# Eleven rows of unused matmuls behind the third weight tile of a two-layer hybrid encoder

## The chip, the cores and the metric

The kernel runs on one core of a Trainium2 chip, in one launch. The metric is the device time in microseconds of that core; lower is better. The engines are PE (matrix multiply; PEld is its loading of weights), DVE and ACT (vector and scalar work), POOL, and SP, which issues the transfers. All of them run their own queue in order and wait for each other by semaphores.

## The reference

Two layers are computed over 528 tokens (16 learned ones ahead of 512) of width 1024. Each layer is a SwiGLU feed forward, a mixer of three groups of heads, and a second SwiGLU feed forward, each with a residual and a layer norm.

```python
def swiglu(h, w_in, w_out):
    gate, up = jnp.split(h @ w_in, 2, axis=-1)
    return (jax.nn.silu(gate) * up) @ w_out
...
    for l in range(DEPTH):
        h = layer_norm(DEEPNORM_ALPHA * h + 0.5 * swiglu(h, w_ff1_in[l], w_ff1_out[l]), ln_g[l, 0], ln_b[l, 0])
        mix = hybrid_mixer(h * valid, w_in[l], w_out[l], ...)
        h = layer_norm(DEEPNORM_ALPHA * h + mix, ln_g[l, 1], ln_b[l, 1])
        h = layer_norm(DEEPNORM_ALPHA * h + 0.5 * swiglu(h, w_ff2_in[l], w_ff2_out[l]), ln_g[l, 2], ln_b[l, 2])
    return h[:, CHUNK:]
```

The mixer runs gated DeltaNet, RWKV-7 and retention heads side by side, all from one input projection, with one output projection. The feed forward has an inner width of 2816, which is 22 blocks of 128.

## The kernel before

The stream lies transposed: features on partitions, tokens along columns. The tokens are worked in two halves, of 272 and of 256 columns (`NH`). A half of the stream is a tile of 128 partitions x 8 blocks x 272 columns; the 256-column half uses 256 of the 272 columns of each block, so its blocks begin 272 columns apart too.

Products are made almost as exactly as in float32 from three matmuls of the type fp32r. Every operand is split by ACT and DVE into a rounded part (`hi`) and the rest (`lo`); ACT writes the first and DVE subtracts. `mm3` (L165) then runs, for each of 8 blocks of the inner dimension, high x high, high x low and low x high: 24 matmuls into one PSUM bank per weight tile. A weight tile is 128 x 1024 floats, 512 KB, loaded by SP into `raw` (4 slots) and split by `load_w` into `whl` (3 slots), in two pieces of 128x512 each on ACT and on DVE. A slot of `whl` comes free when the last matmul that reads it has run.

The units of work of the first feed forward alternate: a `gate` tile, whose result goes through a tanh on ACT (L127) and a product on DVE (L118), and an `up` tile, whose result is multiplied to it and split into `ghi` and `glo`. After eight pairs, eight `ffo` tiles add to the residual. At the start of the program 12 matmuls of ones (`warm`, float32, which appear as 24 in the trace) run, then the first weight tile is loaded and the input with it, four pieces of two blocks each, split as they arrive. `u[0]` is the first unit, and `run_half(u[1:s1], 0)` with `s1 = 3` runs the second and third.

The order of the instructions on each engine isn't written by hand: a tile scheduler places them by its own simulation of the program, with the order of the code as priority, so a unit's matmuls may be placed among those of another. The mixer's small matmuls (`pS`, `pyt`, `pG` and so on, plain float32) are placed among the feed forward's in that way.

Of the kernel before, what the change touches and what calls it, by code (L numbers as in the profile page):

```python
# [14 lines left out]
PSUM = bass.MemoryType.PSUM  # L15
DRAM = bass.MemoryType.DRAM

L = 2
T = 528
NMAX = 272  # L20
NH = (272, 256)
# [5 lines left out]
RSQRT = (-0.49999807, 0.375001003, -0.314047223, 0.273950612)  # L27
# superchunks of a half: (first column, tokens, chunks, tokens per chunk, slot)
SUPERS = (
# [5 lines left out]

# columns of the constants
_C = {}
# [6 lines left out]

# columns of the parameters that lie along partitions
_P = {}
# [13 lines left out]
def body(ctx, tc, xT, w1i, w1o, w2i, w2o, win, wba, wout, par, wsm, wupx, cst, tab, out):  # L60
# [15 lines left out]

    # rings of scratch tiles: (columns, slots); what runs side by side has rings of its own
    RINGS = {
# [53 lines left out]
    def rsqrt(v, n, rows=128, new=TI):  # L132
        """v**-0.5 of a small tile: y from the exponent's halving, within 3.5%, times e**-0.5 for e = v y**2,
        whose polynomial around e = 1 is right to 3e-8."""
        t, y, p = (new(n, x)[:rows] for x in ("rt", "ry", "rp"))
        ts(V, y.bitcast(I32), v.bitcast(I32), -0.5, ALU.mult, float(0x5F3759DF), ALU.add)
        tt(V, t, y, y, ALU.mult)
        tt(V, t, t, v, ALU.mult)
        ts(V, p, t, -1.0, ALU.add, RSQRT[3], ALU.mult)
        ts(V, t, t, -1.0, ALU.add)  # L140
        for c in RSQRT[2::-1]:
            stt(p, p, c, t, ALU.add, ALU.mult)
        stt(y, p, 1.0, y, ALU.add, ALU.mult)
        return y
# [22 lines left out]

    S = {}  # tiles that live across steps

    nh, off = list(NH), [0, 0]  # columns at work, and those of the half before them  # L170

# [6 lines left out]

    # ---------------------------------------------------------------- layer norm
    def add_r(hf, m):  # L180
# [69 lines left out]

    # ---------------------------------------------------------------- feed forward
    def ff_units(l, wi, wo, j, last=False):
        """One unit per weight tile: (tile's source, k-tiles, work of a half)."""
        units = []
# [107 lines left out]

    # ---------------------------------------------------------------- mixer inputs
    def silu2(dst, x, n, src=None):
        """2 * silu(x)"""
        t = ring("ws", n, name="tanh")
        act(t, x, AF.Tanh, scale=0.5)
        stt(dst, t, 1.0, x, ALU.add, ALU.mult)

    def in_units(l):  # L370
# [20 lines left out]
        def conv(i):  # L391
            def run(hf, w):
                n = nh[hf]
                ps = bank(psA, "qkv")[:, :n]
                mm3(ps, w, S["hl", hf], 8)
                p = ring("ws", n + 3, name="pc")
                act(p[:, 3:], ps, AF.Copy)
                if hf == 0:
                    G.memset(p[:, 0:3], 0.0)
                    G.tensor_copy(halo[:, i], p[:, n: n + 3])  # L400
                else:
                    G.tensor_copy(p[:, 0:3], halo[:, i])
                c = ring("ws", n, name="conv")
                c0 = _P["conv"][0] + 4 * i
                act(c, ps, AF.Identity, scale=P[:, c0 + 3: c0 + 4])
                for tap in (0, 1, 2):
                    stt(c, p[:, tap: tap + n], P[:, c0 + tap: c0 + tap + 1], c, ALU.mult, ALU.add)
                # heads' k and q lie side by side
                if i < 4:
                    d = keep(hf, "qk")[:, 2 * i + 1, :n]  # L410
                elif i < 8:
                    d = keep(hf, "qk")[:, 2 * (i - 4), :n]
                else:
                    d = keep(hf, "vz")[:, i - 8, :n]
                silu2(d, c, n)
            return (win[l, i], 8, run)

        def rw(i):
            def run(hf, w):
                n = nh[hf]  # L420
# [14 lines left out]
                if i in (4, 5):  # L435
                    # v: the two chunks of a superchunk change places
                    c = ring("ws", n, name="vmix")
                    act(c, ps, AF.Identity, scale=S["par2"][:, i: i + 1])
                    for s, _, nch, Cn, _ in SUPERS[hf]:
                        for q in range(nch):  # L440
                            a, b = s + q * Cn, s + (nch - 1 - q) * Cn
                            stt(d[:, b: b + Cn], p[:, a: a + Cn], mu, c[:, a: a + Cn], ALU.mult, ALU.add)
                else:
                    act(d, ps, AF.Identity, scale=S["par2"][:, i: i + 1])
                    stt(d, p[:, 0:n], mu, d, ALU.mult, ALU.add)
# [39 lines left out]

    # ---------------------------------------------------------------- inverses of I + M
    def inverse_base(dg, dw, nch, Cn):
        """M: strict upper triangles, four heads' in dg, four in dw; inverses of all eight,
        of the 16-wide blocks on the diagonals here."""
        BS = 16  # L490
# [13 lines left out]

        # blocks on the diagonal, one to a partition
        key = "md" if nch == 2 else "md0"
# [35 lines left out]
    def inverse_levels(out, M, X, Y, nch):  # L542
        """From 16-wide blocks to whole chunks."""
        if Y is None:
# [30 lines left out]

    # ---------------------------------------------------------------- gated DeltaNet
    def gdn_gates(hf, baT):
        """beta and the decays' logarithms with their sums, tokens on partitions."""
        P = S["par"]
# [44 lines left out]
    def gdn_pre(hf, si, d, pool):  # L624
# [27 lines left out]
        yield  # L652
        # q, k and v with tokens on partitions
        nk, nq = TP(4, "nk"), TP(4, "nq")
# [95 lines left out]

    # ---------------------------------------------------------------- norm of 64-wide heads
    def head_norm(py, n, eps, small="ti", big="c1"):
        """py: [n, 4, 64] in PSUM -> normalised, in SBUF"""
        st6 = ring("s6", 24, name="st6")
# [16 lines left out]

    # ---------------------------------------------------------------- RWKV-7
    def rwkv_pre(hf, si, d, pool):
# [12 lines left out]

        # decay
        xw = ring("p1", n, name="xw")
# [16 lines left out]
        yield  # L805
        # in-context learning rate, keys
        pa = bank(pool, "pa")[:, : 2 * n].rearrange("p (j t) -> p j t", j=2)
# [20 lines left out]
        yield  # L828
        # with the decays: k and b over theirs, r and kappa times theirs
        bk = ring("p2", 2, 2 * nch, w, name="bk")  # L830
# [12 lines left out]
        yield  # L843
        # bonus
        rkp = kap
# [8 lines left out]
        yield  # L854
        # products inside a chunk
        Am = []
# [106 lines left out]

    # ---------------------------------------------------------------- retention
    def ret_all(hf, si):
# [40 lines left out]

    # ---------------------------------------------------------------- parameters of a layer
    def load_params(l):
# [9 lines left out]
        S["wba"] = w  # L1018
        # 1 - mu | norm_w / 2 | a0 / 2 | ka / 2 | 1 - ka / 2 | lnx g, b / 2 | ret g, b / 2
        Q = pp.tile([128, 22], F32, name=f"par2{l}")  # L1020
# [19 lines left out]

    # ---------------------------------------------------------------- layers
    def scratch():
# [26 lines left out]
    def turns(*gens):  # L1069
        """Turns of several emissions."""  # L1070
        gens = list(gens)
# [55 lines left out]
    def go(seq):  # L1127
        """Units of either half in turn; a callable is called."""
        for x in seq:
            if callable(x):  # L1130
                x()
            else:
                run_half([x[0]], x[1])
# [4 lines left out]
    def mix(a, b):  # L1138
        """Two sequences in proportion."""
        o, i, j = [], 0, 0  # L1140
# [9 lines left out]
    def warm_up():  # L1150
        G.memset(ones, 1.0)
        p = bank(psL, "warm")
        for i in range(12):
            mm(p[:, :128], ones, ones)

    for l in range(L):
        u = ff_units(l, w1i, w1o, 0)
        last = l == L - 1
        if l == 0:
# [4 lines left out]
            u[0][2](0, w0)  # L1164
            run_half(u[1:s1], 0)
            consts()
            scratch()
# [20 lines left out]
        else:  # L1188
            # the second feed forward of half b runs beside the first of half a
            a0, a1 = 14, 36  # L1190
# [31 lines left out]

# ---------------------------------------------------------------- host: layout only
def _consts():
# [13 lines left out]
    for li, s in enumerate(LEVELS):  # L1238
        # transposed blocks: rows of the second half of a pair, columns of the first
        lv[:, li] = (j64[:, None] // (2 * s) == k[None, :] // (2 * s)) & (j64[:, None] // s % 2 == 1) & (k[None, :] // s % 2 == 0)  # L1240
# [40 lines left out]
def _arrays(inp):  # L1281
# [5 lines left out]

    def cols(w):  # [L, K, n*128] -> [L, n, 128, K/128*128]
        l, K, n = w.shape
# [22 lines left out]

    def along(v):  # [L, n*128] -> [L, 128, n]
        return v.reshape(L, -1, 128).transpose(0, 2, 1)
# [35 lines left out]
```

## Time and profile before

| | |
|---|---|
| time, median of 2 runs | 2451.01 us (2450.98 to 2451.03) |
| profiled execution: span from first to last instruction | 2448.9 us |
| PE busy, share of the span | 2393.6 us, 98% |
| PEld busy | 2291.4 us, 94% |
| DVE busy | 1817.2 us, 74% |
| ACT busy | 1226.6 us, 50% |
| mean granted PE clock | 0.989 |

The profile gives no time of its own for its execution beside the span; the median of the runs is 2.1 us above it. A matmul's duration in the profile reaches from its start to the end of its result, and matmuls overlap, so the sum of durations is more than the time that they hold the engine; the distance from start to start is the number that adds up. The granted clock is 1.00 at 2.4 GHz and 0.50 at 1.2 GHz.

### The profile page before, as it was taken

The page shows a single profiled execution, that of the slowest core. Times are in us where ns is not written, and L with a number is a line of the kernel's source. Part 1 is how long each engine was busy: PE and PEld are TensorE (multiplying, and loading weights), DVE is VectorE, ACT ScalarE, POOL GpSimd, SP SyncE. Part 2 cuts the span into 40 slices and gives each one's busy share as a digit, 9 for nine tenths or more (in the row PEclk, how much of TensorE's full clock was granted, in tenths as well). Part 3 has the DMA queues.
Part 4 walks back from the last instruction along what each step waited for, and adds up shares of the span by engine and source line. Part 5 has one row for each costly group of instructions (what it writes and reads, how often), then busy time and mean ns, then how long its engine had stood idle before and what let it go on. Part 6 is the DMA issues. An engine that isn't in the chain of part 4 may idle for free.

```text
span 2448.9 us, 51826 instructions
## 1 busy us (share of the span) xinstructions
PE 2393.6 (98%) x20058; PEld 2291.4 (94%) x20058; DVE 1817.2 (74%) x4325; ACT 1226.6 (50%) x2813; POOL 293.8 (12%) x492
## 2 busy tenths in 40 slices
PE   9999999999899999999999999999999999999997
PEld 9999999889899989999999998988998989999997
DVE  6668688768888656976667679876687886687667
ACT  5445555434665335554445556633556653355444
POOL 1001112202222000300001003210022220010002
PEclk9999999999999999999999999999999999999998
DMA  7655554424544525555555544343455445255554
GB/s 247 207 166 176 177 168 133 127 89 157 174 155 150 145 87 176 179 166 181 181 181 172 188 159 147 118 125 103 166 169 185 158 141 154 95 192 171 194 169 127
DMA packets 169822, 389.24 MB, mean 159 GB/s; under 512 B 63751, under 2 KB 79721, under 8 KB 168937
## 3 DMA queue, kind: packets, MB, share of 16 engines
q1 hardware_dynamic: 169576, 385.94, 48.7%
q8 instruction: 158, 2.59, 0.4%
q14 instruction: 88, 0.71, 0.1%
HBM read 372.01 MB, written 13.88 MB: 158 GB/s over the span
## 4 chain that ended last, share of the span: by engine, by line
PE 89%; DVE 6%; ACT 2%; issue 1%; POOL 1%; DMA 1%; SPq 0%; POOLq 0%; ACTq 0%; DVEq 0%
PE ffo L165 21%; PE up L165 20%; PE gate L165 20%; PE qkv L165 5%; PE rw L165 3%; PE out L165 3%; PE rt L165 3%; DVE whl L115 2%; PE po L130 1%; DVE h L118 1%; PE z L165 1%; PE pR L130 1%; PE pyr L130 1%; PE pS L130 1%; PE px L130 1%
## 5 line engine op out<-in xcount | busy, mean ns | idle before, releaser
L127 ACT ACTIVATE whl<-raw 128x512 fp32r<-128x512 f32 x1384 | 780.3, 614 | 618.4 <-issue 221.6
L115 DVE TENSOR_TENSOR whl<-raw,whl 128x512 fp32r<-128x512 f32 x1384 | 940.3, 710 | 97.2 <-ACT whl L127 84.3
L165 PE MATMUL gate<-hi,whl 128*128 128x256 f32 (+1 forms) x2816 | 554.6, 287 | 7.1 <-DVE m L118 5.1
L165 PE MATMUL up<-hi,whl 128*128 128x256 f32 (+1 forms) x2816 | 553.9, 287 | 1.7 <-DVE m L115 1.2
L165 PE MATMUL ffo<-ghi,whl 128*128 128x256 f32 (+1 forms) x2816 | 529.7, 286 | 5.4 <-DVE h L118 5.2
L165 PEld LDWEIGHTS gate<-hi,whl 128*128 128x128 f32 x2816 | 450.6, 189 | 14.6 <-DVE m L118 6.1
L165 PEld LDWEIGHTS up<-hi,whl 128*128 128x128 f32 x2816 | 451.2, 190 | 7.4 <-issue 3.8
L165 PEld LDWEIGHTS ffo<-ghi,whl 128*128 128x128 f32 x2816 | 440.3, 188 | 11.8 <-DVE h L118 6.4
L165 PE MATMUL up<-lo,whl 128*128 128x256 f32 (+1 forms) x1408 | 403.7, 287 | 0.0
L165 PE MATMUL gate<-lo,whl 128*128 128x256 f32 (+1 forms) x1408 | 402.9, 286 | 0.6 <-DVE lo L115 0.5
L165 PE MATMUL ffo<-glo,whl 128*128 128x256 f32 (+1 forms) x1408 | 399.1, 284 | 0.0
L165 PEld LDWEIGHTS gate<-lo,whl 128*128 128x128 f32 x1408 | 266.1, 189 | 3.6 <-issue 1.6
L165 PEld LDWEIGHTS up<-lo,whl 128*128 128x128 f32 x1408 | 266.7, 189 | 2.6 <-issue 1.2
L165 PEld LDWEIGHTS ffo<-glo,whl 128*128 128x128 f32 x1408 | 264.9, 188 | 0.9 <-issue 0.2
L127 ACT ACTIVATE tanh<-gate 128x256 f32<-128x256 f32 (+1 forms) x176 | 68.1, 387 | 231.7 <-PE gate L165 231.5
L118 DVE SCALAR_TENSOR_TENSOR m<-tanh,gate 128x256 f32<-128x256 f32 (+1 forms) x176 | 74.6, 424 | 141.0 <-ACT tanh L127 140.0
L118 DVE SCALAR_TENSOR_TENSOR h<-ffo,h 128x256 f32<-128x256 f32 (+1 forms) x192 | 81.5, 427 | 98.9 <-PE ffo L165 98.2
L165 PE MATMUL qkv<-hi,whl 128*128 128x272 f32 (+1 forms) x768 | 152.3, 290 | 1.6 <-ACT rk L127 1.6
L115 DVE TENSOR_TENSOR m<-m,up 128x256 f32<-128x256 f32 (+1 forms) x176 | 74.5, 423 | 94.8 <-PE up L165 94.1
L165 PEld LDWEIGHTS qkv<-hi,whl 128*128 128x128 f32 x768 | 122.4, 189 | 4.4 <-ACT rk L127 2.4
L165 PE MATMUL qkv<-lo,whl 128*128 128x272 f32 (+1 forms) x384 | 109.3, 285 | 0.0
L165 PE MATMUL out<-yhi,whl 128*128 128x256 f32 (+1 forms) x512 | 95.7, 285 | 4.6 <-DVE h L118 3.1
(316 smaller groups left out, 3280.0 us busy)
## 6 DMA issues: line engine op xcount, KB each, us to landing
raw<-w1i SPq DMA_DIRECT2D x176, 512.0 KB, 3.4
raw<-w2i SPq DMA_DIRECT2D x176, 512.0 KB, 3.3
raw<-win SPq DMA_DIRECT2D x116, 512.0 KB, 3.3
raw<-w1o SPq DMA_DIRECT2D x64, 512.0 KB, 3.3
raw<-w2o SPq DMA_DIRECT2D x64, 512.0 KB, 3.3
raw<-wout SPq DMA_DIRECT2D x32, 512.0 KB, 4.3
raw<-w1o SPq DMA_DIRECT2D x32, 384.0 KB, 3.0
raw<-w2o SPq DMA_DIRECT2D x32, 384.0 KB, 3.0
```

Source lines behind the costliest of these rows:

```text
L115: e.tensor_tensor(out=o, in0=a, in1=b, op=op)
L118: V.scalar_tensor_tensor(out=o, in0=a, scalar=s, in1=b, op0=op0, op1=op1)
L127: A.activation(out=o, in_=a, func=f, **kw)
L130: PE.matmul(o, lhsT=l, rhs=r, start=start, stop=stop)
L165: PE.matmul(ps, lhsT=w[:, a, k, :m], rhs=x[b][:, k, :n], start=(i == 0), stop=(i == 3 * nk - 1))
```

## The change

A function `widths` is added and called once, behind the third unit of the first layer. It takes the first weight tile `w0`, both parts, and the split stream of the first half as one row of 2176 columns, and runs eleven groups of 24 matmuls (264 in all) into the bank of the pool `psL`, in the same pattern of high and low parts as `mm3`. The groups differ in the number of columns (128, 256, 264, 272, 288, 384, 512), in where the moving columns begin, and in whether the weights change from block to block (`one=True` keeps block 0). Nothing reads the results. Comments and docstrings are taken out of the file as well, which moves no instruction.

```diff
+    def widths(w):
+
+        hi, lo = (t.rearrange("p k t -> p (k t)") for t in S["hl", 0])
+
+        def run(n, at, name, m=128, one=False, cnt=24):
+            p = bank(psL, name)[:m, :n]
+            for i in range(cnt):
+                x = (hi, lo)[i % 3 == 1]
+                k = 0 if one else i // 3 % 8
+                PE.matmul(p, lhsT=w[:, int(i % 3 == 2), k, :m], rhs=x[:, at(i // 3 % 8): at(i // 3 % 8) + n],
+                          start=i == 0, stop=i == cnt - 1)
+
+        run(256, lambda k: 272 * k, "w256a")
+        run(256, lambda k: 256 * k, "w256b")
+        run(256, lambda k: 272 * k, "w256c", one=True)
+        run(256, lambda k: 0, "w256d")
+        run(272, lambda k: 272 * k, "w272")
+        run(512, lambda k: 512 * (k % 4), "w512a")
+        run(512, lambda k: 512 * (k % 4), "w512b", one=True)
+        run(384, lambda k: 384 * (k % 4), "w384")
+        run(288, lambda k: 288 * (k % 6), "w288")
+        run(264, lambda k: 264 * (k % 8), "w264")
+        run(128, lambda k: 128 * k, "w128")
...
             load_x(0)
             u[0][2](0, w0)
             run_half(u[1:s1], 0)
+            widths(w0)
             consts()
             scratch()
```

The scheduler spreads the added matmuls. On PE at the start of the program, where `gate` is the first weight tile, the order before was this:

```order
L130 MATMUL warm<-ones 128x128 x12
L165 MATMUL gate<-hi,whl 128x272
L165 MATMUL gate<-lo,whl 128x272
L165 MATMUL gate<-hi,whl 128x272 x2
L165 MATMUL gate<-lo,whl 128x272
```

and at the same place it is now:

```order
L130 MATMUL warm<-ones 128x128 x12
L165 MATMUL gate<-hi,whl 128x272
L1165 MATMUL w256a<-hi,whl 128x256
L165 MATMUL gate<-lo,whl 128x272
L165 MATMUL gate<-hi,whl 128x272 x2
L165 MATMUL gate<-lo,whl 128x272
L165 MATMUL gate<-hi,whl 128x272 x2
L1165 MATMUL w256a<-lo,whl 128x256
L1165 MATMUL w256a<-hi,whl 128x256 x2
```

One matmul of the first added group stands behind the first gate matmul, and six more behind the next six of them; 18 of the 24 lie among the first tile's, five behind the first two `up` matmuls, one behind the second tile. The other groups stand whole, behind or inside the tiles that follow. On PE behind the third tile (a `gate`), where the fourth (an `up`) came next:

```order
L165 MATMUL gate<-hi,whl 128x272
L1165 MATMUL w256b<-hi,whl 128x256
L1165 MATMUL w256b<-lo,whl 128x256
L1165 MATMUL w256b<-hi,whl 128x256 x2
...
L1165 MATMUL w256b<-hi,whl 128x256
L165 MATMUL up<-hi,whl 128x272
L165 MATMUL up<-lo,whl 128x272
L165 MATMUL up<-hi,whl 128x272 x2
```

The second group of 24 now lies between the third and the fourth tile; the last group, of 128 columns, lies inside the eleventh tile. Later on the order is as before except for one stretch of PE, DVE and ACT in the first mixer, in which the same instructions are interleaved in another way. On PE, around the matmuls `pS` (a state's update) at 550 us of the trace of before:

```order
 L165 MATMUL up<-hi,whl 128x256 x2
 L165 MATMUL up<-lo,whl 128x256
+L165 MATMUL up<-hi,whl 128x256 x2
+L165 MATMUL up<-lo,whl 128x256
+L165 MATMUL up<-hi,whl 128x256 x2
 L130 MATMUL pS<-vh,kd 128x128 x4
-L165 MATMUL up<-hi,whl 128x256 x2
-L165 MATMUL up<-lo,whl 128x256
-L165 MATMUL up<-hi,whl 128x256 x2
```

`pS` now stands five `up` matmuls later.

## Rows read from the trace of the kernel before

**Rows 1.** The page's head and parts 1 and 2: busy time, granted clock in slices.

```profile
span 2448.9 us, 51826 instructions
...
PE 2393.6 (98%) x20058; PEld 2291.4 (94%) x20058; DVE 1817.2 (74%) x4325; ACT 1226.6 (50%) x2813; POOL 293.8 (12%) x492
...
PEclk9999999999999999999999999999999999999998
```

**Rows 2.** The page's part 4, shares of the chain that ended last.

```profile
PE 89%; DVE 6%; ACT 2%; issue 1%; POOL 1%; DMA 1%; SPq 0%; POOLq 0%; ACTq 0%; DVEq 0%
```

**Rows 3.** PE's waits, whole span: total us, times, longest us.

```profile
PE pvar L130 <- DVE sq L115: 5.3, 1, 5.3
PE ffo L165 <- DVE h L118: 5.2, 9, 2.6
PE gate L165 <- DVE m L118: 5.1, 5, 1.7
```

**Rows 4.** Stretch 10.6 to 40 us: length, PE busy (matmuls), clock, DMA share, GB/s.

```profile
10.60:40.00 29.40, 29.40 (x233) 1.00 0.82 283
```

**Rows 5.** The chain in order of time, first half: start us, us, what.

```profile
16.65 3.03 PE up L165 x24
19.68 3.03 PE gate L165 x24
```

**Rows 6.** The same chain, second half.

```profile
574.60 2.84 PE gate L165 x24
577.44 2.84 PE up L165 x24
```

**Rows 7.** The same chain, plain f32 matmuls of 512 columns.

```profile
422.08 0.86 PE pG L130 x2
```

**Rows 8.** PE's timeline near 357 us: start us, us, instructions.

```profile
356.92 1.00 PE L130 MATMUL pyt<-vk,at 128*128 128x64 f32 x8
357.75 0.65 PE L130 MATMUL pSt<-vk 128*128 128x256 f32 x2
```

**Rows 9.** PE's timeline from 5 to 11.5 us.

```profile
5.87 0.39 PE L165 MATMUL gate<-hi,whl 128*128 128x272 f32 x1 [0.22 <-ACT hi L127]
6.77 0.39 PE L165 MATMUL gate<-lo,whl 128*128 128x272 f32 x1 [0.50 <-DVE lo L115]
...
7.37 0.41 PE L165 MATMUL gate<-hi,whl 128*128 128x272 f32 x2
7.85 0.40 PE L165 MATMUL gate<-lo,whl 128*128 128x272 f32 x1
8.09 0.41 PE L165 MATMUL gate<-hi,whl 128*128 128x272 f32 x2
...
10.23 0.29 PE L165 MATMUL up<-lo,whl 128*128 128x272 f32 x1
10.59 0.52 PE L165 MATMUL up<-hi,whl 128*128 128x272 f32 x2
10.94 0.28 PE L165 MATMUL up<-lo,whl 128*128 128x272 f32 x1
```

**Rows 10.** Groups by shape, 0 to 40 us: count, busy us, mean ns, idle before.

```profile
L115 DVE TENSOR_TENSOR whl<-raw,whl 128x512 fp32r<-128x512 f32 x26 | 16.8, 687 | 8.7 <-ACT whl L127 8.4
L127 ACT ACTIVATE whl<-raw 128x512 fp32r<-128x512 f32 x26 | 14.9, 623 | 10.0 <-DMA raw<-w1i 5.3 <-issue 3.3 <-PE up L165 1.5
```

**Rows 11.** Stretches of 530 to 600 us: busy time by engine, clock, DMA.

```profile
540.00:550.00 10.00, 10.00 (x84) 8.57 (x83) 4.60 (x10) 4.39 (x11) 0.00 (x0) 1.00 0.16 52
550.00:560.00 10.00, 10.00 (x79) 8.80 (x77) 6.91 (x16) 3.50 (x8) 0.72 (x1) 1.00 0.31 95
```

**Rows 12.** Two of eight stretches with a lower clock: length, PE busy, clock.

```profile
235.00:250.00 15.00, 13.25 (x100) 0.89 0.59 205
...
2430.00:2448.90 18.90, 3.99 (x20) 0.63 0.17 56
```

## The prediction, made before the changed kernel ran

> **What bounds the kernel now.** I read the page first, then the chain, the waits of the matrix engine, and its rows near the start. The page [rows 1] shows PE busy for 2393.6 of 2448.9 us, so there are 55.3 us without a matmul, and a granted clock of at least nine tenths in 39 of 40 slices. The chain that ended last [rows 2] is PE for 89% of the span; no other engine has more than 6%. What PE waits for [rows 3] is a set of small results that other engines make from PE's own output (a variance, a residual, a gated product), the longest 5.3 us. None is a wait for weights once the start is over: from 10.6 to 40 us PE is busy for all of 29.40 us at clock 1.00 [rows 4]. A matmul that is put there therefore has no hole to fall into. It moves every later one back by its own pitch, from start to start. So the price of this change is a sum of pitches, less what falls into the waits before 10.6 us.
>
> **Pitches that the trace shows.** Durations in the page are no help, since matmuls overlap. The chain gives pitches directly. The half of 272 columns runs 24 matmuls of a weight tile in 3.03 us [rows 5], which is 126.3 ns each; the half of 256 columns takes 2.84 us [rows 6], or 118.3 ns. Divided by columns that is 0.464 and 0.462 ns, nearly the same, and about a tenth more than the 0.417 ns of one column per clock at 2.4 GHz. I read the tenth as belonging to the column, not to the instruction, since 8.0 ns for 16 more columns leaves nothing over for a constant. These matmuls have the same operand types as the added ones (the high and low parts of weights and of the stream).
>
> **The added matmuls, row by row.** There are eleven rows of 24.
> Four rows of 256: 96 x 118.3 = 11.36 us. Where the columns start (steps of 272, of 256, or always at 0) and whether the weights change, I price at nothing: both halves of the program read at steps of 272 already, and a weight load lies beside each matmul in any case.
> One row of 272: 24 x 126.3 = 3.03 us. One of 264, midway: 24 x 122.3 = 2.94 us. One of 288, at 0.463 ns a column: 24 x 133.3 = 3.20 us.
> One row of 384: 24 x 177.8 = 4.27 us. Two rows of 512: 48 x 237.1 = 11.38 us. No row of the trace has this kind so wide. The lower end is half of the plain f32 row of 512 columns, 430 ns each [rows 7], as that form takes two clocks a column: 215 for 512 and 161 for 384, which takes off 1.06 and 0.40 us. The upper end is a line through 118.3 and 126.3, which gives 246 and 182 ns and adds 0.5 us in all. I take the rate per column, because two widths agree on it.
> One row of 128: here the weight load can be what lasts. Eight f32 matmuls of 64 columns with 128-column weights take 0.83 us from the first start to the next tile's [rows 8], 104 ns each, though 64 columns at two clocks each need 53. I take 104, which gives 24 x 104 = 2.50 us; at 0.463 ns a column it would be 59, 1.07 us less. A gain is excluded for all of these, as each one occupies PE's queue.
> The sum is 11.36 + 3.03 + 2.94 + 3.20 + 4.27 + 11.38 + 2.50 = 38.7 us, with ends of 36.1 and 39.2.
>
> The 272-column pitch of 126.3 ns [rows 5] bears on a rule for the wide rows. The Trainium skill, "TensorE: Matmul & The Clock Gate", section "Back-to-back issue gap", gives an isolated gap of the column count over 2.4 GHz plus 2.5 ns. By that rule 272 columns would take 115.8 ns, and the sum would be 35.7 us with 104 ns kept for the narrow row; the trace disagrees at the two widths that it has. The same section gives about 81 ns for a stream of loads and matmuls of 128 columns, by which the narrow row would be 0.6 us cheaper; rows 8 speak against it.
>
> **What the start hides.** The scheduler does not leave the first row behind the third tile: it puts 18 of the 24 into the first tile's work and five between the first matmuls of the second. In the trace of before [rows 9] PE has gaps there. After the first gate matmul the next comes 0.90 us later, and one added matmul of 0.12 us fits in. The matmul at 7.85 comes 0.22 us after its turn (7.37 plus two pitches) and the restart costs 0.11 more. The up matmul at 10.59 comes 0.23 us after its turn, and its restart costs 0.11 again. Six added matmuls of 0.71 us stand ahead of the 7.85 one, so both of these gaps are filled. That hides 0.12 + 0.33 + 0.34 = 0.8 us, between 0.1 and 1.0 if the restarts behave otherwise. Nothing is late next: in before, the up matmuls of the second tile run from 10.59 on, so its weights are there, and the added ones bring PE to that place only after 11 us.
>
> **The weight ring.** The extra matmuls keep the first tile's pair in its slot, so of three slots two are left while they last. Splitting a tile takes two ACT pieces of 0.62 us and two DVE pieces of 0.69 [rows 10], about 2.0 us from start to end as they overlap. A slot comes free when its tile's 24 matmuls end, and its next user starts at least 3.03 us later, since another tile and mostly 24 added ones lie between. I price it at nothing; without that cover PE would wait once for about 1.4 us, the first ACT and DVE pieces. The one moved DMA on SP (a weight tile issued ahead of four zero fills of scratch) costs nothing: those fills are needed only in the first mixer, hundreds of microseconds later. ACT's split of the third tile now stands ahead of the first tile's tanh, which delays only a product that is used a tile later: also nothing.
>
> **What moves later.** Everything behind is 37.9 us later in the same order, except between about 530 and 600 us, where the scheduler interleaves the mixer's small matmuls differently with the feed forward. PE is full in that stretch before, and DVE is not [rows 11]; I take 0, with -0.5 to +1.5 us. The granted clock falls to the lower level in eight short stretches, where PE waits, one of them at the end; near 240 us it is 0.89 over 15 us [rows 12], which is 3.3 us at half speed, at most 1.7 us of delay. A delay of 38 us may shift, add or drop such a stretch: plus or minus 1.7 us.
>
> So the forecast is 38.7 - 0.8 = 37.9 us, a span of 2486.8. The runs of before have a median of 2451.0, 2.1 us more than the span, which stays. The time is **2488.9 us**, 1.5% longer. A measurement of this kernel can tell about 2% from no change, so this counts as within it.
>
> **The rivals.** First, slower by over 2%: beyond some width the moving operand is read at two clocks a column, as the f32 row of 512 is [rows 7]. At 430 ns the two rows of 512 cost 9.3 us more, and at 323 ns the row of 384 costs 3.5 more: 50.7 us in all, 2501.7. It decides from 49 us of added time, so nearly all three wide rows must be hit. Against it: 256 and 272 columns show no step, and the two-clock rows are of another type.
> Second, not slower: the added work replaces waits, because the 55.3 us of holes could close when the helpers have run ahead, or because unused results were dropped. That would give about 2451. Against it: the 264 matmuls stand in PE's program, and the waits [rows 3] hang on PE's own latest results, so they move with it; the rings hold only a few tiles.
> Third, cheaper: the tenth above one column per clock comes from traffic of the working stage and not from the columns. At half of rows 7, 0.42 ns a column, the sum is 35.3 - 0.8 = 34.5 us and the time 2485.5. For it: plain f32 of 512 columns has no such excess. Against it: it holds at both widths and all through the program.
>
> **How the numbers follow.** The forecast with its own ends has 0.78, the cheaper rival 0.12, the two-clock rival 0.06, the not-slower rival 0.03 and a larger shift of clock stretches 0.01. The low end takes 36.1 us, a cover of 1.0, -1.7 for the clock and -0.5 for the order: 32.9, or 2484. The high end takes 39.2 less 0.1, +1.7 and +1.5: 42.3, or 2493. That holds the forecast and the cheaper rival. Over 2% slower begins at 2500.0: only the two-clock rival gets there, 0.06. Over 2% faster has no mechanism, 0.01. The rest is 0.93.
>
> **What would show it.** In the changed profile the added rows should stand without idle time before them. The pitches of 256 and 272 should be 118 and 126, that of 512 near 237 and that of 128 near 104. PE's busy time should grow by about 39 us and the idle time by nothing, and the tiles behind the last added row should start some 38 us late, with the lag kept to the end. A pitch of 430 at 512 columns, or a lag that shrinks after the first layer, would prove me wrong.

## The result, and the profile after

The changed kernel took 2492.4 us (median of 2 runs, 2490.18 and 2494.62) against 2451.01: 1.0174 times the time before, with a 95% interval of 1.0156 to 1.0192. The forecast was 2488.9 us in a range of 2484 to 2493. So the size came out 3.5 us higher than forecast, inside the range, but the step that turned it into "counts as within it" was wrong: a slowdown of 1.7% is a clear result here, as the experiments on the scatter of runs show below. The added matmuls' results are read by nobody, and the output is the same.

The page of the changed kernel, its head and parts 1 to 4:

```profile
span 2492.7 us, 52357 instructions
...
PE 2433.9 (98%) x20322; PEld 2330.7 (93%) x20322; DVE 1818.5 (73%) x4325; ACT 1225.8 (49%) x2813; POOL 290.4 (12%) x492
...
PEclk9999999999999999999999999999999999999998
...
PE 87%; DVE 8%; DMA 2%; ACT 1%; issue 1%; POOL 1%; SPq 0%; POOLq 0%; ACTq 0%; DVEq 0%
```

Beside [rows 1, 2]: the span grew by 43.8 us. PE's busy time grew by 40.3 and its idle time by 3.5, from 55.3 to 58.8. This profiled execution was one of the longer ones (2494.62), so the traces differ by 43.8 us where the medians differ by 41.4.

The chain in order of time has the added rows as pieces (start us, us, what). "w" are the rows of 272, 384, 288, 264 and 128 columns, in that order:

```profile
7.77 0.70 PE w256a L1165 x6
...
18.63 2.87 PE w256b L1165 x24
...
24.03 2.84 PE w256c L1165 x24
...
29.39 2.88 PE w256d L1165 x24
...
34.79 3.03 PE w L1165 x24
...
40.34 5.45 PE w512a L1165 x24
...
48.32 5.46 PE w512b L1165 x24
...
56.30 4.19 PE w L1165 x24
...
63.01 3.19 PE w L1165 x24
...
68.72 2.90 PE w L1165 x24
...
74.14 2.63 PE w L1165 x24
```

Only the first row is in six pieces, 2.7 to 2.8 us together. The eleven sum to 38.25 us; 38.7 was forecast. From 49.00 to 78.40, a stretch as long as that of [rows 4], PE has no idle time:

```profile
49.00:78.40 29.40, 29.40 (x212) 28.57 (x211) 7.92 (x15) 5.85 (x13) 0.00 (x0) 1.00 0.22 72
```

PE's timeline where [rows 9] had its gaps shows added matmuls in them:

```profile
5.86 0.39 PE L165 MATMUL gate<-hi,whl 128*128 128x272 f32 x1
6.09 0.28 PE L1165 MATMUL w256a<-hi,whl 128*128 128x256 f32 x1
6.75 0.39 PE L165 MATMUL gate<-lo,whl 128*128 128x272 f32 x1 [0.39 <-DVE lo L115]
...
7.61 0.28 PE L1165 MATMUL w256a<-lo,whl 128*128 128x256 f32 x1
...
8.31 0.29 PE L165 MATMUL gate<-lo,whl 128*128 128x272 f32 x1
```

How late a matmul comes can be read from the same instruction in both timelines. The one of [rows 8] stands 37.55 us later:

```profile
394.47 1.00 PE L130 MATMUL pyt<-vk,at 128*128 128x64 f32 x8
```

Done for every matmul, this lag is 37.48 us from 80 to 200 us of before, so against this one trace of before the start hid 38.25 - 37.48 = 0.8, as forecast. The lag is 37.9 at 520 us and 38.45 at 600, behind the stretch where the order is another. Then it leaves the forecast's path: 38.6 at 800 us, 40.3 at 845, 43.9 at 1005, and 43.8 at the end. PE's waits name both jumps (total us, times, longest us):

```profile
PE gate L165 <- DVE m L118: 5.9, 5, 1.8
PE ffo L165 <- DVE h L118: 5.9, 11, 2.6
PE pvar L130 <- DVE sq L115: 5.3, 1, 5.3
...
PE pz L130 <- DMA Y<-xd: 1.9, 2, 1.6
```

The last line has no counterpart in the trace of before. The chain there (start us, us, what) goes through two transfers of the second layer's mixer:

```profile
840.51 4.09 DMA xd<-XB
844.60 0.02 issue
844.62 3.93 DMA Y<-xd
848.55 0.14 issue
848.68 0.30 PE pz L130 x2
```

In before the same place of the chain is PE alone:

```profile
798.97 9.46 PE ffo L165 x75
808.42 0.26 PE pz L130 x2
```

The second jump: ACT waits 4.01 us for the transfer h<-hd, four conversions then stand ahead of the tanh, and PE waits 1.80 us for the product behind it (timelines of ACT and of PE):

```profile
992.64 0.63 ACT L127 ACTIVATE hi<-h 128x512 fp32r<-128x512 f32 x1 [4.01 <-DMA h<-hd]
...
997.14 0.38 ACT L127 ACTIVATE tanh<-gate 128x272 f32<-128x272 f32 x1
```

```profile
995.95 0.29 PE L165 MATMUL up<-hi,whl 128*128 128x272 f32 x1
998.04 0.42 PE L165 MATMUL gate<-hi,whl 128*128 128x272 f32 x1 [1.80 <-DVE m L118]
998.27 0.42 PE L165 MATMUL gate<-lo,whl 128*128 128x272 f32 x1
998.49 0.66 PE L165 MATMUL gate<-hi,whl 128*128 128x272 f32 x2
```

Behind that wait the matmuls stand 0.23 us apart instead of 0.126: the granted clock is at the lower level for 3.4 us, which costs 1.7 more. Wait and clock make the 3.5 us. In before ACT waited 1.35 us for this transfer and PE had no wait there.

### The profile page after: what moved, and what is told of

Same layout as the page of the kernel before. It is cut to its first block, busy times and chain, and to the rows that moved or that the text cites. A ratio compares the mean times of both kernels' runs of the same rounds, so it can differ in the third digit from the quotient of the medians.

```text
span 2492.7 us, 52357 instructions
## 1 busy us (share of the span) xinstructions
PE 2433.9 (98%) x20322; PEld 2330.7 (93%) x20322; DVE 1818.5 (73%) x4325; ACT 1225.8 (49%) x2813; POOL 290.4 (12%) x492
## 4 chain that ended last, share of the span: by engine, by line
PE 87%; DVE 8%; DMA 2%; ACT 1%; issue 1%; POOL 1%; SPq 0%; POOLq 0%; ACTq 0%; DVEq 0%
PE gate L165 19%; PE ffo L165 19%; PE up L165 19%; PE qkv L165 6%; PE rw L165 3%; PE out L165 3%; PE rt L165 2%; DVE whl L115 2%; PE po L130 1%; DVE h L118 1%; PE z L165 1%; PE pR L130 1%; PE pyr L130 1%; PE pS L130 1%; DVE lo L118 1%
```

## The experiments

Each was timed beside runs of the kernel before on the same chip. All 47 runs of before together have a mean of 2450.6 us with a standard deviation of 2.8; that the first two agreed to 0.05 us was chance. So single executions differ by more than the terms in dispute, which are therefore read from the traces, and totals from means.

### e1_null and e2_again: how much do executions differ?

No edit: the kernel before, and the changed kernel.

> The kernel before once more, under a name of its own, to see how far two programs with the same instructions differ. If the 1 to 5 us that the changed kernel took beyond its added matmuls are chance (stretches of lower clock, a transfer that lands late), runs of this kernel should scatter too: 2451 with single runs up to 2455, ratio 0.999 to 1.001. If they are an effect of the change, all runs stay at 2451.0 within 0.5 us.

> The changed kernel unchanged, five rounds. In the first profile the lag behind the last added matmul was 37.5 us and grew to 43.8 by the end. Theory of chance: the lag at 41 us is 37.5 again, the end lag differs, the times lie between 2488 and 2495 with a median near 2490. Rival, a fixed cost of the delay (order in the first mixer, phase of the clock): end lag 43 to 44 again and all times within 1 us of 2494.

Before: 2449.64 us (2445.72 to 2452.73, 11 runs), ratio 0.9996 [0.9987, 1.0005]. Changed: 2491.84 us (2487.8 to 2493.24, 4 runs), ratio 1.0166 [1.0152, 1.0179]. A measurement here tells 0.1% from nothing. The six runs of the changed kernel have a mean of 2491.6, 40.9 us over before with an error of about 1.1.

Executions of one program already differ at the start. e1_null is 1.45 us behind the trace of before from 9 us on, because PE waits longer for the pieces of the input. This is one of its waits, in before and then in e1_null (total us, times, longest us):

```profile
PE gate L165 <- DVE lo L115: 0.5, 1, 0.5
```

```profile
PE gate L165 <- DVE lo L115: 1.1, 3, 0.5
```

So a lag against a single trace of before is uncertain by about 1 us.

Most of the scatter of the totals goes with the clock. Each run lists its span and its mean granted clock; the span times the missing share of the clock is the time that the run lost to it, 23.0 us on average in the 45 runs of before that list it. From run to run of before, 1 us more of it goes with 0.82 us more time (correlation 0.86). The six runs of the changed kernel lost 25.7 us, 2.7 more with an error of 1.3. At 0.82 that is 2.2 of their 40.9 us.

The trace of the second execution of the changed kernel (e2_again) has a lag of 37.9 behind the rows, the rise between 520 and 600 us again (0.54), the wait of 1.6 for Y<-xd again and one of 0.5 behind h<-hd, and it ends 37.0 us late. The difference to the 43.8 above is mostly clock: ahead of the last stretch, which all have, the lower clock takes 44.4 us of the first changed execution, 23.9 of the second, 37.5 of before and 23.9 of e1_null.

### e3_later: the same rows in a place without gaps

```diff
-            widths(w0)
...
-            run_half(u[s1:s2], 0)
+            run_half(u[s1:20], 0)
+            w20 = load_w(*u[20][:2])
+            u[20][2](0, w20)
+            widths(w20)
+            run_half(u[21:s2], 0)
```

> The same eleven rows moved behind the twenty-first weight tile, and reading that tile, where PE has no gaps. If the start hid 0.8 us, nothing is hidden here: the lag behind the rows is 38.3 us, 0.8 more than with the rows at the start, time about 2451.0 + 38.3 = 2489.3 plus the same scatter. Rival, that the start hid nothing and the rows themselves are cheaper: lag 37.5 here too.

2492.03 us (2488.45 to 2494.7, 5 runs), ratio 1.0165 [1.0151, 1.0178]. The rows cost what they cost at the start (chain, start us, us, what):

```profile
72.01 2.81 PE w256a L1165 x24
...
99.00 5.46 PE w512a L1165 x24
...
114.95 4.16 PE w L1165 x24
...
132.77 2.63 PE w L1165 x24
```

The lag is 0.7 us ahead of them and 38.9 behind them, so the rows add 38.2 us: their sum of pitches, with nothing hidden. For the rows at the start the lag is 37.5 to 37.9. What the start hid depends on how late the start would have been without them, which is 0, 0.7 and 1.45 us in the traces of before, e3 and e1_null: something between 0.4 and 2.2 us. The total can't show it (41.0 over the mean of before, with an error of 1.3).

### e4_double: twice the matmuls

```diff
-        def run(n, at, name, m=128, one=False, cnt=24):
+        def run(n, at, name, m=128, one=False, cnt=48):
```

> Each row has 48 matmuls where it had 24. If the added time is the sum of pitches and no more, the lag behind the last row is 2 x 38.25 - 0.8 = 75.7 us and the time 2526.7 plus the scatter of a few us. Rival, a further cost that grows with the delay (5 us on 38 in the first profile): 2451 + 2 x 43.8 = 2538.6.

2529.92 us (2527.13 to 2532.57, 4 runs), ratio 1.0323 [1.0309, 1.0338]. The lag behind the rows is 75.95 us, 38.5 more for a second set of 38.25. The mean is 79.3 us over before, 2.7 more than the rows and the step at 600 us, with an error of 1.5; for the changed kernel that remainder is 2.9, with an error of 1.1. A remainder that grows with the number of added matmuls is not seen.

### e5_shift8, e6_shift1 and e7_a256: nearly nothing added, and eight matmuls fewer

The first two leave one row, of 8 matmuls or of 1; the third has 256 added matmuls instead of 264.

```diff
e5: +        run(256, lambda k: 272 * k, "w256a", cnt=8)     (the only row)
e6: +        run(256, lambda k: 272 * k, "w256a", cnt=1)     (the only row)
e7: -        run(128, lambda k: 128 * k, "w128")
    +        run(128, lambda k: 128 * k, "w128", cnt=16)
```

> Only 8 added matmuls of 256 columns, 0.95 us of PE, most of it in gaps of the start. The scheduler then interleaves the first mixer in the other way, as in the changed kernel, and all later PE instructions lie 16 places further in the instruction stream. If the 3 to 4 us that the changed kernels took beyond the sum of pitches come from the order and from where instruction fetches fall, they are here too: 2450.1 + 0.2 + 3 = about 2453, a lag that steps up by 0.55 us near 600 us, and a PE wait for the transfer Y<-xd of 1 us or more near 810 us. Rival, that they come from the amount of added work: 2450.3, no such wait.

> One added matmul of 256 columns in a gap of the start; the order of everything else is that of the kernel before. Both theories: no change, 2450.1 within the scatter, no step near 600 us. A wait for Y<-xd near 810 us here would speak against both, and for chance.

> 256 added matmuls in place of 264 (the row of 128 columns has 16), that is 512 PE instructions, a whole number of fetches of 256, so the later fetches fall where they fall in the kernel before. If the place of the fetch makes B<-md land late near 785 us, it lands after about 4.1 us here, as before, PE does not wait for Y<-xd, and the time is 2450.1 + 36.6 + 0.6 = 2487.3. Rival, that the fetch has no part in it: landing after 5 to 6.5 us and a wait of 1 to 1.6 us as in the changed kernel, about 2490.

e5: 2452.53 us (2443.98 to 2458.68, 12 runs), ratio 1.0004 [0.9994, 1.0014]. e6: 2449.91 us (2442.35 to 2456.21, 12 runs), 1.0001 [0.9988, 1.0014]. e7: 2486.55 us (2485.82 to 2487.84, 4 runs), 1.0146 [1.0133, 1.016].

The order near 560 us: e6 keeps the order of before and has no rise of the lag there; e5 has the changed kernel's order there and, with 8 added matmuls, a rise of 0.57 us. So do the others of that order, 0.54 to 0.59 in all ten traces with it. This price belongs to the order.

The late transfers: e5 has one of them,

```profile
PE pz L130 <- DMA Y<-xd: 1.6, 1, 1.6
```

and e7, with nearly all of the added work, has neither. Its chain at that place is PE, as in before (start us, us, what):

```profile
829.04 14.82 PE ffo L165 x116
843.86 0.10 issue
843.96 0.30 PE pz L130 x2
```

The expectation named another transfer, B<-md, ahead of these two. From issue to landing it took 4.0 and 4.2 us in before and e1_null, 4.2 in e7, and 5.7 and 6.5 in the two traces of the changed kernel, as expected; but in e5, with a late Y<-xd, it took 4.1. So a late B<-md is not what makes Y<-xd late.

Eight matmuls less, 0.9 us, took 4.9 us off the mean (2486.7 against 2491.6). That is no measure of the jumps: e7's runs lost 4.0 us less to the clock than the changed kernel's, which at 0.82 accounts for 3.3, and e7 also has another order later on. Apart from the added rows, PE's order is the changed kernel's in all kernels with added matmuls but e6 as far as 1500 us of before. Between 1537 and 1637 us e3, e5, e7, e9 and e11 have another, and e4 one of its own; e2 and e10 alone have the changed kernel's from end to end. What e5 and e7 show stands in their traces: e5 has one of the jumps with 8 added matmuls, and e7 has neither with 256. So the jumps do not follow the amount that is added.

### e8_pitch: what the tenth above one column per clock belongs to

In place of the eleven rows stand others, for a profile alone (one execution of 2500.69 us): 512 columns as in the change; with 8 and with 32 weight columns; each matmul closed for itself; one part of the weights and stream only; two banks in turn; plain f32; bf16 weights and columns; and narrow rows. Their results are unused as well.

```diff
+                ...
+                elif dt == BF:
+                    l_, r_ = wb[:, :m], rb[:, :n]
+                PE.matmul(ps[i % banks], lhsT=l_, rhs=r_, start=alone or i < banks, stop=alone or i >= cnt - banks)
+        run("qm8", m=8)
+        run("qbf", dt=BF)
+        ...
```

> Other rows of 24 in the same place, to see what the 11 to 14 ns above one column per clock hang on; 512 columns each, 227.2 ns in the changed kernel. Weights of 8 or of 32 columns in place of 128: about 216 if the weight load makes the excess, 227 if not. Every matmul alone instead of accumulating: 216 if accumulation makes it. Two banks in turn: 216 if the bank does. One part of the stream only: 216 if changing between parts does. The same operands as plain f32: 430 each pass. bf16 of ones: 216 if the 4-byte type makes it, 227 if any moving operand has it. 64 columns with 128-column weights: 110, the load; 128 columns with 8-column weights: 65.

The median distance from start to start, in ns:

| 512 columns | ns | narrow | ns |
|---|---|---|---|
| as in the change | 227 | 128 columns, 8 weight columns | 60 |
| 8, 32 weight columns | 227, 232 | 128 columns, 128 weight columns (changed kernel) | 112 |
| closed each; one part; two banks | 227, 227, 227 | 64 columns, 128 weight columns | 112 |
| bf16 | 216 | bf16, 128 columns | 56 |
| plain f32, each of two passes | 429 | | |

Rows of its chain (start us, us, what), with the 8-weight-column row first and the bf16 row and the 8-weight-column row of 128 columns behind it:

```profile
27.14 5.45 PE qm L1175 x24
...
74.59 1.36 PE qbf L1175 x24
...
78.39 1.44 PE qm8n L1175 x24
```

At one column per clock, 512 columns are 213.3 ns and 128 are 53.3. bf16 is 2.7 above that at both; the kernel's type is 14 above at 512 and 7 at 128. Neither the weights' width nor accumulation, banks or parts take the excess away, and bf16 operands do. They differ from the others in type and also in value (all ones), and no row tells these two apart, so the type is the likely cause and not a shown one. With 128 weight columns the narrow rows of the kernel's type are at 112 with 128 and with 64 columns, and with 8 weight columns at 60: there the width of the weights sets the distance.

The Trainium skill, "TensorE: Matmul & The Clock Gate", section "Back-to-back issue gap", gives the column count over 2.4 GHz plus 2.5 ns for the gap of a single matmul, an estimate of 215.8 and 55.8 here: the bf16 rows agree, and the kernel's type, at 227 and 60, does not.

### e9_n384, e10_n392 and e11_n320: are instruction transfers what makes Y<-xd late?

PE's instructions come in transfers of 16 KB in a queue of their own (the page's part 3 of the changed kernel: packets, MB, share):

```profile
q8 instruction: 160, 2.62, 0.4%
```

Before has 158; 264 matmuls with their weight loads made it 160 and twice as many 162, which fits 256 instructions in each. In the traces so far, such a transfer came 1.3 to 3.6 us after the issue of xd<-XB wherever Y<-xd was late, and at about 5 us, behind it, where it was not. If the place follows from the number of added instructions, 768 (a multiple of 256, as e7's 512) should be in time, 784 late, and 640 in time.

```diff
-        run(128, lambda k: 128 * k, "w128")
+        run(128, lambda k: 128 * k, "w128", cnt=144)     (e10: 152, e11: 80)
```

> The rows of the changed kernel with the 128-column one lengthened from 24 to 144 matmuls: 384 added matmuls, 768 instructions on PE, three full instruction transfers of 256. Both theories expect a lag of 37.5 + 120 x 0.1096 = 50.6 us behind the added rows and 51.2 behind the other order near 600 us. Fetch theory (the late Y<-xd of the second mixer comes from an instruction transfer that meets the small transfers xd<-XB; which it does depends on how the added instructions stand to a full 256): from the issue of xd<-XB to that of Y<-xd 3.6 to 4.0 us as before, no wait of PE for Y<-xd over 0.5 us, lag at 841 us about 51.5. Rival (the other order, or any added work, makes it late): a wait of 1.5 us and a lag of 52.8 or more.

> The same with 152 instead of 144 matmuls of 128 columns: 392 added, 784 instructions, 16 over a full multiple of 256, as in the changed kernel. Lag behind the rows 37.5 + 128 x 0.1096 = 51.5 us. Fetch theory: 4.8 to 5.5 us from the issue of xd<-XB to that of Y<-xd, a wait of PE for Y<-xd of 1.0 to 1.7 us, so that eight more matmuls, 0.88 us, come out as 2.0 to 2.5 us of lag at 841 us. Rival (order or amount): the two kernels differ by 0.88 us alone and both wait, or neither does.

> The same with 80 matmuls of 128 columns: 320 added, 640 instructions, half of an instruction transfer off. Lag behind the rows 37.5 + 56 x 0.1096 = 43.6 us. Fetch theory: the instruction transfer comes some 7 us away from xd<-XB, so that Y<-xd is issued 3.6 to 4.0 us after it and PE waits for less than 0.5 us. Rival (any amount that is no multiple of 256 instructions, or the other order): a wait of 1.0 to 1.7 us.

e9: 2501.41 us (2500.89 to 2508.7, 4 runs), ratio 1.0216 [1.0193, 1.0238]. e10: 2504.32 us (2500.23 to 2506.26, 4 runs), 1.0215 [1.0193, 1.0238]. e11: 2493.09 us (2491.28 to 2498.75, 4 runs), 1.0179 [1.0157, 1.02].

All programs, from their traces, in us (for h<-hd from its issue to ACT's use of it; the last column is the rise of the lag from 800 to 1005 us):

| kernel | added on PE | issue of xd<-XB to that of Y<-xd | instruction transfer, after the first | PE waits for Y<-xd | h<-hd | PE waits behind it | lag's rise |
|---|---|---|---|---|---|---|---|
| before, e1 | 0 | 3.6, 3.7 | 4.7, 4.7 | 0, 0 | 6.2, 6.6 | 0, 0 | 0, 0 |
| e6 | 2 | 3.9 | 5.4 | 0.4 | 6.6 | 0 | 0.4 |
| e7 | 512 | 3.8 | 5.0 | 0 | 6.7 | 0 | 0.1 |
| e5 | 16 | 5.1 | 1.8 | 1.6 | 6.7 | 0 | 3.1 |
| changed, e2 | 528 | 4.8, 5.5 | 1.6, 1.7 | 1.6, 1.6 | 8.9, 7.6 | 1.8, 0.5 | 5.3, 2.4 |
| e3 | 528 | 5.0 | 1.5 | 1.5 | 7.1 | 0 | 3.4 |
| e4 | 1056 | 4.9 | 1.3 | 0.9 | 8.5 | 1.5 | 2.7 |
| e10 | 784 | 4.8 | 2.1 | 0.9 | 8.6 | 1.6 | 2.9 |
| e9 | 768 | 5.5 | 3.0 | 1.2 | 7.8 | 0.8 | 2.3 |
| e11 | 640 | 4.4 | none near | 0.5 | 8.7 | 1.7 | 2.5 |
| e8 | 504 | 6.1 | 3.6 | 1.6 | 8.5 | 1.5 | 3.4 |

e10 came about nearly as the fetch theory has it (4.8 us, with a wait of 0.9 where 1.0 to 1.7 was expected), and e11 is nearer to it than to its rival, though its 4.4 us are over the 3.6 to 4.0 expected. e9 missed: the transfer came at 3.0 and Y<-xd late, so the number of added instructions does not give its place. What still holds in all thirteen traces is the observation: 4.8 us or more with an instruction transfer in the first 3.6 us, at most 4.4 without. It is a coincidence seen thirteen times, not a cause shown by an edit. For h<-hd there is no such pattern: e11 is late with no instruction transfer near.

## Why the prediction was right and wrong

**The bound: right.** PE had no hole. The rows stand in the chain without idle time, and the lag was kept to the end: 43.8 us in the first trace, and in the second 37.9 behind the rows and 37.0 at the end.

**The sum of pitches: right, 38.25 against 38.7.** The 256, 264, 272 and 288 columns came within 0.1 us a row (118 to 120, 121, 126 and 133 ns), and place and repeated weights made no difference, as priced. The step "I read the tenth as belonging to the column, not to the instruction" failed: e8 and the wide rows have a nearly constant 11 to 14 ns from 256 columns on. The rate per column made 512 columns 237 where they took 227 (0.47 us over two rows) and 384 columns 178 where they took 175. The narrow row was 110 where 104 was taken, 0.13 us the other way. The two-clock rival is dead: no wide row shows a step. The cheaper rival's size is wrong as well. It was right that the tenth is not in the columns, but the traffic that it named isn't shown as the reason: the bf16 rows of e8 stand in the same stage and have 2.7 ns.

**What the start hides: right in kind, its size not shown.** 0.8 us was forecast and 0.8 is read against the trace of before, but that they agree is luck: against e3's start it would be 1.5 and against e1_null's 2.2. **The weight ring: right**, no wait for weights.

**"What moves later ... I take 0, with -0.5 to +1.5": mis-sized.** The other order near 560 us costs 0.55, inside its bounds. "Everything behind is 37.9 us later in the same order" missed a term, and "the idle time by nothing" with it (PE's grew by 3.5 us): in the second mixer two small transfers, xd<-XB and h<-hd, land later against PE's work, and PE waits for what hangs on them. In the traces with added work the lag rises there by 2.3 to 5.3 us, except in e6 (0.4) and e7 (0.1); how much of this the means show stands below. The row for it was to be had. In before, ACT already waited for h<-hd (its timeline):

```profile
949.68 0.63 ACT L127 ACTIVATE hi<-h 128x512 fp32r<-128x512 f32 x1 [1.35 <-DMA h<-hd]
```

That is 6.2 us after the issue; the table has no wait of PE at 7.1 us and one of 0.5 at 7.6, so the slack was about 0.9 us.

**Clock, plus or minus 1.7: too narrow for one execution.** The traces of one and the same kernel differ by 13.6 and 20.5 us of lower clock, which is up to 7 and 10 us of time, and less where PE waits anyway: e1_null's span is 3.3 us under that of before, e2_again's 6.8 under the first changed one. Nor do six runs average it out: it holds 2.2 of their 40.9 us.

**"A measurement of this kernel can tell about 2% from no change, so this counts as within it": failed, and with it the chances.** No run shows the 2%: the two runs then known agreed to 0.05 us. The forecast of +37.9 us was 1.5%, and runs of this kernel tell 0.1 to 0.2%: e5 and e6, with at most 1 us added, have intervals of 0.1% around 1, and the changed kernel's interval begins at 1.0156. The 0.93 for no change should have stood for slower. The argument itself (a sum of pitches on a full PE, no gain possible) had no case near zero but the not-slower rival at 0.03, and that one is dead too: PE's busy time grew by 40.3 us.

**What stays open.** Of the 40.9 us that six runs measured, the rows take 37.5, the order 0.55 and the lower clock 2.2, which leaves 0.7 us, less than the uncertainty of the start. The other kernels come out the same way. Less rows and order, e3, e4, e5, e7, e9, e10 and e11 have remainders of 1.6, 2.7, 0.8, -1.5, 0.7, 0.5 and -1.1 us, with errors of 0.9 to 1.5. Less 0.82 us for each us that their runs lost to the clock beyond before, they have 0.0, -0.2, 0.3, -0.4, -0.4, 0.4 and -1.1. So the waits for late transfers, though the traces of all of these but e7 have 1 to 3 us of them, leave nothing of that size in the means; how often an execution pays them isn't settled. Whether the change itself makes the lower clock more frequent isn't either: e4's runs lost 3.5 us more to it than those of before, e7's 1.3 less. What makes the transfers late is open too; taking away the neighbouring weight transfers, which all programs have there too, was not tried.

## What to carry to other kernels

Work added to a full engine costs its pitches, and rows of the trace gave that sum within 2%; in single traces the rest came from the clock and from places far behind the edit where a result lands just in time, so look for waits of another engine that are nearly long enough to reach the bound one. Whether such a wait is paid in most executions is read from the totals, and those are compared only after their granted clocks. Before calling a small forecast "no change", ask how far runs of the same kernel differ: a 1.5% sum with no way down is a slowdown, and two runs that agree don't tell the scatter. To price a wider matmul than the trace has, take one column per clock plus the constant seen at the widths it has; 12 ns from 256 and 272 columns would have given 225 at 512 and 172 at 384, where 227 and 175 were measured.

## What had not been expected of the hardware

The excess over one column per clock is 3 ns for the bf16 rows and 7 to 14 ns for this kernel's type, whatever the weights' width, the banks or the accumulation. An instruction transfer of 16 KB for PE coincides with small transfers that land 1 to 2 us later. The mean granted clock of a run accounts for most of the scatter between executions of one program (0.82 us of time for each us lost, correlation 0.86). And of the eleven waits of PE of 1.2 to 1.8 us in the two places of the table, three were followed by 3.4 us at the lower clock level (1.8 us in the first changed execution, 1.6 in e5, 1.5 in e3), which doubles the price of such a wait; the other eight, of the same lengths, were not.
